# Seven block products in three of eight K pairs instead of two, with one block sum made by an accumulating transfer

## The chip, the cores and the metric

The kernel runs on one core of one Trainium2 chip. The metric is device time in microseconds (us), the median of the runs shown; lower is better. The core has a matrix engine (PE, with its weight loads shown as PEld), a vector engine (DVE), a scalar engine (ACT), a general engine (POOL) and a sequencer that mostly issues transfers (SP). Each engine works through its own instructions in order and waits on semaphores for the others.

## What is computed

Two decoder layers over 256 tokens of width 2048: a state-space mixer in the first, differential attention in the second, and after each a SwiGLU feed-forward network (FFN) with 5632 hidden columns, all with RMSNorm before and after. The change lies in the gate and up products of the FFN:

```python
def swiglu(h, w_gate, w_up, w_down):
    return (jax.nn.silu(h @ w_gate) * (h @ w_up)) @ w_down
...
    for i in range(DEPTH):
        ...
        h = rmsnorm(x, norm_ffn_pre[i])
        x = x + rmsnorm(swiglu(h, ffn_w_gate[i], ffn_w_up[i], ffn_w_down[i]), norm_ffn_post[i])
```

## The kernel before, in words

All weights come from HBM as float32. PE multiplies float32r, so each block of weights is split on the way: ACT casts it to `hi` (line 119), DVE subtracts to get `lo` (line 120), and a product is three matmuls: x_hi by hi, x_hi by lo, x_lo by hi.

**Where the blocks live.** A `raw` tile holds four blocks of 128x512 (1 MB) and there are three of them; `hi` and `lo` have four tiles each in the FFN. SP issues the loads in order and stops at one whose `raw` tile is still in use.

**The FFN.** Hidden columns come in chunks of 512. Chunk 10 is done by the plain routine `mv`. The other ten go two at a time through `pair`, once for gate (`wg`) and once for up (`wu`), so each FFN calls `pair` ten times and the kernel twenty times. The calls lie in three parts: one gate and up, then two, then two; each part is followed by its share of the down product (`out_proj`). What `pair` computes is a 2x2 grid of results: two token halves t by two column chunks c, each a PSUM accumulator `acc` (four banks). Its K dimension of 2048 is walked in eight K pairs kp = 0..7; each loads the 2x2 weight blocks (two K blocks by two chunks), and each of the four results needs two products of 128x128 by 128x512.

**The seven.** For the K pairs named in `SEVEN` the eight products are replaced by seven, after Strassen's scheme in Winograd's form. The block sums of x are made once per FFN by `make_forms` and kept in `xr` tiles (four); they are read through `form`. The sums of weight blocks are made per K pair: three raw blocks are split first (`prep(raw[:, 1:4])`), then DVE makes four sums in place of the raw blocks (lines 239 to 242, each 128x512), then the tile is split again (`prep(raw)`), giving `sh` and `sl`. Four of the seven products collect in banks of their own (`p1`, `p5`, `p6`, `p7`, tile name `cp`, from the four `aux` banks), the other three go straight into `acc`. After the last K pair of `SEVEN`, DVE combines the four (lines 257 to 260), and at the end of the pair `done` adds each to its `acc` and frees the bank (lines 743, 752, 753).

**What sets the order.** A scheduler places each engine's instructions by the order in which the kernel names them and by when tiles come free; `later` and `tick` delay some work by a number of steps. So the order of DVE and SP around a pair's end is not written in the source.

Of the kernel before, what the change touches and what calls it, by code (L numbers as in the profile page):

```python
# [10 lines left out]
F32 = mybir.dt.float32  # L11
F32R = mybir.dt.float32r
AF = mybir.ActivationFunctionType
ALU = mybir.AluOpType
AX = mybir.AxisListType

P = 128
S = 256
NT = 2
# [10 lines left out]
LAG = 4  # L30
LAG2 = 2

SEVEN = (3, 5)


@with_exitstack
def trunk_kernel(ctx, tc, x_rows, x_cols, vec_cols, vec64, post_rows, lam_rows,
                 w_zxbc, w_dt, w_so, w_qkv, w_ao,
                 w_g0, w_u0, w_d0, w_g1, w_u1, w_d1, out):
    nc = tc.nc  # L40
# [99 lines left out]
    def later(k, fn):  # L140
        deferred.append((step_no[0] + k, fn))
# [6 lines left out]
    def lookup(dct, key):  # L148
        while key not in dct:
            deferred.popleft()[1]()  # L150
        return dct[key]
# [49 lines left out]
    def pair(blocks, seven, form, done):  # L201

        flush()
        acc = {}  # L210
        end = len(blocks) - 1

        def mm(k, st, hi, lo, last):
            first = k not in acc
            if first:
                acc[k] = (auxp.tile([P, 512], F32, tag="aux", name="cp") if isinstance(k, str) else
                          accp.tile([P, 512], F32, tag="acc", name="acc"))
            for q, (a, b) in enumerate(((st[0], hi), (st[0], lo), (st[1], hi))):
                nc.tensor.matmul(acc[k], a, b, start=first and q == 0, stop=last and q == 2)  # L219

        ss = {}
        for kp, src in enumerate(blocks):
            raw = rawp.tile([P, 4, 512], F32, tag="raw", name="raw")
            for c in range(2):
                nc.sync.dma_start(raw[:, 2 * c:2 * c + 2], src[c])
            if kp not in seven:
                hi, lo = prep(raw)
                for t in range(NT):
                    for c, e in ((0, 2), (1, 0)):
                        for j in range(2):  # L230
                            mm((t, c), x_stat(2 * kp + j, t), hi[:, e + j], lo[:, e + j], kp == end and j == 1)
                        if kp == end:
                            done(t, c, acc[(t, c)], ss)
                    tick()
                continue
            last = kp == seven[-1]
            hi, lo = prep(raw[:, 1:4])

            nc.vector.tensor_tensor(raw[:, 2], raw[:, 2], raw[:, 0], op=ALU.add)
            nc.vector.tensor_tensor(raw[:, 0], raw[:, 0], raw[:, 1], op=ALU.add)  # L240
            nc.vector.tensor_tensor(raw[:, 1], raw[:, 1], raw[:, 2], op=ALU.add)
            nc.vector.tensor_tensor(raw[:, 3], raw[:, 3], raw[:, 1], op=ALU.add)
            sh, sl = prep(raw)
            k0, k1 = 2 * kp, 2 * kp + 1
            mm("p1", x_stat(k0, 0), hi[:, 1], lo[:, 1], last)
            mm((0, 0), x_stat(k1, 0), hi[:, 2], lo[:, 2], False)
            mm((0, 1), form(kp, 3), hi[:, 0], lo[:, 0], False)
            tick()
            mm("p6", form(kp, 2), sh[:, 1], sl[:, 1], last)
            mm("p5", form(kp, 0), sh[:, 2], sl[:, 2], last)  # L250
            mm("p7", form(kp, 1), sh[:, 0], sl[:, 0], last)
            mm((1, 0), x_stat(k1, 1), sh[:, 3], sl[:, 3], False)
            tick()
            if last:
                s1, u, w, x = (t512(n) for n in ("s1", "su", "sw", "sx"))
                nc.scalar.copy(s1, acc["p1"])
                nc.vector.tensor_tensor(u, acc["p6"], s1, op=ALU.subtract)
                nc.vector.tensor_tensor(w, acc["p5"], u, op=ALU.add)
                nc.vector.tensor_tensor(u, acc["p7"], u, op=ALU.add)
                nc.vector.tensor_tensor(x, acc["p7"], w, op=ALU.add)  # L260
                ss.update({(0, 0): (s1, ALU.add), (0, 1): (w, ALU.add), (1, 0): (u, ALU.subtract), (1, 1): (x, ALU.add)})

    def split(dst_hi, dst_lo, src):
        nc.scalar.copy(dst_hi, src)
        nc.vector.tensor_tensor(dst_lo, src, dst_hi.bitcast(F32), op=ALU.subtract)
# [399 lines left out]
    def t512(name, shape=(P, 512)):  # L665
        return t5.tile(list(shape), F32, tag="t512", name=name)
# [11 lines left out]

    def xr_tile(name):
        return postp.tile([P, 2, 512], F32, tag="xr", name=name, bufs=4)

    def fetch_x(src):
        for t in range(NT):
# [16 lines left out]
    def ffn(wg, wu, wd, step, final):  # L702
        acts, gt, forms = {}, {}, {}

        def rs(t):
            return lookup(rstd, (step - 1, t))

        def g_evac(t, ps):
            gt[(t, 10)] = t512("g")
            nc.scalar.activation(gt[(t, 10)], ps, AF.Silu, scale=rs(t))  # L710

        def u_evac(t, ps):
            g = gt[(t, 10)]
            nc.vector.scalar_tensor_tensor(g, ps, rs(t), g, op0=ALU.mult, op1=ALU.mult)
            acts[(t, 10)] = act_piece(g, f"f{step}_10_{t}")

        def make_forms(n):

            xf = []
            for t in range(NT):  # L720
                xf.append(t512("xf", (P, 4, P)))
                sl = slice(t * P, (t + 1) * P)
                nc.vector.tensor_tensor(xf[t], xT_hi[n][:, :, sl].bitcast(F32), xT_lo[n][:, :, sl].bitcast(F32), op=ALU.add)
            fa, fb = (t512("f", (P, 2, 2, P)) for _ in range(2))
            nc.vector.tensor_tensor(fa[:, 0], xf[1][:, 0:4:2], xf[1][:, 1:4:2], op=ALU.subtract)
            nc.vector.tensor_tensor(fa[:, 1], xf[1][:, 0:4:2], xf[0][:, 0:4:2], op=ALU.subtract)
            nc.vector.tensor_tensor(fb[:, 0], xf[0][:, 0:4:2], fa[:, 0], op=ALU.subtract)
            nc.vector.tensor_tensor(fb[:, 1], xf[0][:, 1:4:2], fb[:, 0], op=ALU.subtract)
            fh = postp.tile([P, 4, 2, P], F32R, tag="xr", name="fh", bufs=4)
            fl = postp.tile([P, 4, 2, P], F32R, tag="xr", name="fl", bufs=4)  # L730
            for k, f in enumerate((fa, fb)):
                split(fh[:, 2 * k:2 * k + 2], fl[:, 2 * k:2 * k + 2], f)
            forms[n] = (fh, fl)

        def form(kp, f):
            fh, fl = lookup(forms, kp // 2)
            return fh[:, f, kp % 2], fl[:, f, kp % 2]

        def g_done(p):
            def done(t, c, ps, ss):  # L740
                g, op = ss[(t, c)]
                gt[(t, 2 * p + 1 - c)] = g
                nc.vector.tensor_tensor(g, ps, g, op=op)
                nc.scalar.activation(g, g, AF.Silu, scale=rs(t))
            return done

        def u_done(p):
            def done(t, c, ps, ss):
                ch = 2 * p + 1 - c
                g = gt[(t, ch)]  # L750
                y, op = ss[(t, c)]
                nc.vector.tensor_tensor(y, ps, y, op=op)
                nc.vector.scalar_tensor_tensor(g, y, rs(t), g, op0=ALU.mult, op1=ALU.mult)

                def piece():
                    acts[(t, ch)] = act_piece(g, f"f{step}_{ch}_{t}")
                later(2, piece)
            return done

        def twos(w, c):  # L760
            return [[w[c + e, kp // 2, :, kp % 2 * 2:kp % 2 * 2 + 2] for e in range(2)] for kp in range(8)]

        mv([wg[10, k] for k in range(4)], u_stat, g_evac, LAG)
        for t in range(NT):
            rs(t)
            for h in range(2):
                nc.sync.dma_start(xr_d[t][h].rearrange("p (e k) -> p e k", e=2), xr_of[(t, h)])
        for k, n in enumerate(sorted({kp // 2 for kp in SEVEN})):
            later(1 + 3 * k, lambda n=n: make_forms(n))
        mv([wu[10, k] for k in range(4)], u_stat, u_evac, LAG2)  # L770
        parts = [(10, 0, 1), (2, 3, 4, 5), (6, 7, 8, 9)]
        for pi, part in enumerate(parts):
            for c in part:
                if c < 10 and c % 2 == 0:
                    pair(twos(wg, c), SEVEN, form, g_done(c // 2))
                    pair(twos(wu, c), SEVEN, form, u_done(c // 2))
            last = pi == len(parts) - 1
            if last:
                fetch_x(lambda t, h: xr_d[t][h].rearrange("p (e k) -> p e k", e=2))
            out_proj(wd, pi == 0, last, acts, [2 * c + e for c in part for e in range(2)], step, final, LAG2, t512,  # L780
                     load_post(step) if last else None)

    ffn(w_g0, w_u0, w_d0, 1, False)


# [182 lines left out]
```

## Time and profile before

| what | value |
|---|---|
| median of 3 runs | 2602.59 us (2600.7 to 2604.3) |
| the profiled execution, its own time | 2600.35 us |
| its span from first to last instruction | 2598.3 us |
| PE busy | 2561.4 us, 99% of the span |
| DVE busy | 1815.8 us, 70% |
| ACT busy | 1276.9 us, 49% |
| POOL busy | 158.4 us, 6% |
| DMA of the load queue | 489.27 MB, 53.3% of 16 engines' span |
| granted PE clock | 0.995 |

A timeline row of the profile gives start, duration, engine, line, operation, what it writes and reads, and in brackets how long the engine stood idle before it and who ended that. A row of groups ends in: busy us, mean ns of one, then idle us of the engine before them with the releasers. A row of waits gives total us, how often, and the longest. Rows of windows give the length, then busy us and (count) of PE, PEld, DVE, ACT and POOL, then the granted clock, the DMA share and GB/s. A matmul's duration in the trace includes its passage through the array, so matmuls overlap: their step is read from their starts.

### The profile page before, as it was taken

To read this page: it belongs to the slowest core of one execution; us is meant where nothing else is said; L and a number is where in the kernel's file an instruction comes from. 1 tells how busy PE (TensorE), PEld (TensorE's weight loads), DVE (VectorE), ACT (ScalarE), POOL (GpSimd) and SP (SyncE) were. 2 spreads that over 40 slices of the span, in tenths; PEclk is the share of its full clock that TensorE was granted. 3 is DMA by queue.
4 is the path that set the end of the run, shared out by engine and by line. 5 is a ranking of instruction groups with operands and counts; after the bars stand their busy time and mean duration, and the time that the engine had idled before them with its cause. 6 is when DMAs were issued, how large, how long until landed. Compare 5 with 4: busy or idle time off the path is not lost.

```text
span 2598.3 us, 31297 instructions
## 1 busy us (share of the span) xinstructions
PE 2561.4 (99%) x12270; PEld 2105.6 (81%) x12270; DVE 1815.8 (70%) x2230; ACT 1276.9 (49%) x1506; POOL 158.4 (6%) x164
## 2 busy tenths in 40 slices
PE   8999999999999999999999999999999999999998
PEld 7878888888878888888888788887788888888886
DVE  7888757887687567846785666556577478657864
ACT  4555655555564444534453554445554444434442
POOL 2021000111100000000001100001100000000001
PEclk9999999999999999999999999999999999999999
DMA  6545554544754654655465544444555555555563
GB/s 223 189 142 201 183 194 174 194 167 162 267 214 163 222 199 162 220 187 202 168 243 203 189 145 167 174 157 144 212 188 207 179 203 189 203 181 191 198 231 137
DMA packets 111699, 492.10 MB, mean 189 GB/s; under 512 B 10880, under 2 KB 27584, under 8 KB 75712
## 3 DMA queue, kind: packets, MB, share of 16 engines
q1 hardware_dynamic: 110896, 489.27, 53.3%
q8 instruction: 96, 1.57, 0.2%
q10 hardware_dynamic: 656, 0.85, 0.1%
q14 instruction: 51, 0.42, 0.0%
HBM read 483.71 MB, written 6.36 MB: 189 GB/s over the span
## 4 chain that ended last, share of the span: by engine, by line
PE 86%; DVE 6%; issue 3%; ACT 2%; DMA 2%; POOL 0%; DVEq 0%; SPq 0%; ACTq 0%; POOLq 0%
PE acc L168 39%; PE acc L219 23%; PE acc L193 11%; PE acc L195 6%; PE cp L219 3%; DVE lo L120 2%; ACT hi L119 2%; PE sc L844 1%; DMA raw<-in_w_d_dram 1%; DMA raw<-in_w_g_dram 1%; PE py L498 1%; DVE v L423 1%; PE pt_f L271 1%; PE ptx L574 0%; PE pyt L508 0%
## 5 line engine op out<-in xcount | busy, mean ns | idle before, releaser
L120 DVE TENSOR_TENSOR lo<-raw,hi 128x2048 fp32r<-128x2048 f32 (+2 forms) x528 | 1030.4, 1961 | 609.2 <-ACT hi L119 608.8
L119 ACT CAST hi<-raw 128x2048 fp32r<-128x2048 f32 (+2 forms) x528 | 851.1, 1618 | 924.8 <-PE acc L168 250.4
L219 PE MATMUL acc<-hi,xT 128*128 128x512 f32 x2080 | 656.8, 390 | 0.0
L193 PE MATMUL acc<-xT,hi 128*128 128x512 f32 x1280 | 456.6, 401 | 0.0
L219 PEld LDWEIGHTS acc<-hi,xT 128*128 128x128 f32 x2080 | 390.5, 188 | 80.5
L219 PE MATMUL acc<-lo,xT 128*128 128x512 f32 x1040 | 405.0, 389 | 0.0
L195 PE MATMUL acc<-xT,lo 128*128 128x256 f32 x1280 | 359.7, 282 | 5.8 <-DVE lo L120 5.8
L168 PE MATMUL acc<-hi,xT 128*128 128x512 f32 x1024 | 334.9, 399 | 2.3 <-ACT xT L579 2.0
L193 PEld LDWEIGHTS acc<-xT,hi 128*128 128x128 f32 x1280 | 241.8, 189 | 57.1 <-issue 0.9
L168 PE MATMUL acc<-hi,ah_f 128*128 128x512 f32 x704 | 274.8, 390 | 0.0
L168 PE MATMUL acc<-lo,ah_f 128*128 128x512 f32 x704 | 274.6, 390 | 0.0
L168 PE MATMUL acc<-hi,al_f 128*128 128x512 f32 x704 | 273.8, 389 | 0.0
L195 PEld LDWEIGHTS acc<-xT,lo 128*128 128x128 f32 x1280 | 243.4, 190 | 8.3 <-DVE lo L120 6.7
L168 PEld LDWEIGHTS acc<-hi,xT 128*128 128x128 f32 x1024 | 191.8, 188 | 48.1 <-issue 5.1
L219 PEld LDWEIGHTS acc<-lo,xT 128*128 128x128 f32 x1040 | 195.3, 188 | 40.2
L168 PE MATMUL acc<-lo,xT 128*128 128x512 f32 x512 | 206.7, 404 | 1.6 <-DVE lo L120 1.6
L168 PEld LDWEIGHTS acc<-hi,ah_f 128*128 128x128 f32 x704 | 132.2, 188 | 27.3
L168 PEld LDWEIGHTS acc<-hi,al_f 128*128 128x128 f32 x704 | 132.2, 188 | 27.0
L168 PEld LDWEIGHTS acc<-lo,ah_f 128*128 128x128 f32 x704 | 132.2, 188 | 26.9
L600 POOL TENSOR_TENSOR m<-m,wpost 128x512 f32<-128x512 f32 x24 | 44.2, 1842 | 1462.8 <-ACT junk L282 1423.2
L124 DVE SCALAR_TENSOR_TENSOR lo<-raw,cols,hi 128x512 fp32r<-128x512 f32 x128 | 92.7, 771 | 52.0 <-ACT hi L123 51.7
L168 PEld LDWEIGHTS acc<-lo,xT 128*128 128x128 f32 x512 | 96.4, 188 | 23.7 <-issue 3.9
(251 smaller groups left out, 2701.0 us busy)
## 6 DMA issues: line engine op xcount, KB each, us to landing
raw<-in_w_d_dram SPq DMA_DIRECT2D x88, 1024.0 KB, 4.8
raw<-in_w_zxbc_dram SPq DMA_DIRECT2D x80, 1024.0 KB, 4.8
raw<-in_w_g_dram SPq DMA_DIRECT2D x160, 512.0 KB, 4.4
raw<-in_w_u_dram SPq DMA_DIRECT2D x160, 512.0 KB, 4.7
raw<-in_w_qkv_dram SPq DMA_DIRECT2D x48, 1024.0 KB, 4.7
raw<-in_w_so_dram SPq DMA_DIRECT2D x32, 1024.0 KB, 4.7
raw<-in_w_ao_dram SPq DMA_DIRECT2D x16, 1024.0 KB, 4.7
mt<-acum_d SPq DMA_DIRECT2D x16, 512.0 KB, 6.9
```

The source lines that it names most:

```text
L119: nc.scalar.copy(hi, raw)
L120: nc.vector.tensor_tensor(lo, raw, hi.bitcast(F32), op=ALU.subtract)
L124: nc.vector.scalar_tensor_tensor(lo[:, j], raw[:, j], scale[j], hi[:, j].bitcast(F32), op0=ALU.mult, op1=ALU.subtract)
L168: nc.tensor.matmul(acc[t], a, b[:, j], start=(i == 0 and j == 0 and q == 0), stop=(i == last and j == 1 and q == 2))
L193: nc.tensor.matmul(acc[ct], hi[:, j, cs], x.rearrange("p a s -> p (a s)"), start=(i == 0 and j == 0), stop=False)
L195: nc.tensor.matmul(acc[ct][:, :S], lo[:, j, cs], x[:, 0], start=False, stop=(i == last and j == 1))
L219: nc.tensor.matmul(acc[k], a, b, start=first and q == 0, stop=last and q == 2)
L271: nc.tensor.transpose(pt[:, j], src[:, j * P:(j + 1) * P], ident)
L423: nc.vector.scalar_tensor_tensor(v, u[:, k:k + S], cwh[:, ch, k:k + 1], v, op0=ALU.mult, op1=ALU.add)
L498: nc.tensor.matmul(py[e * 64:(e + 1) * 64, a], xd[c][:, 2 * a + e], mts[c][:, 2 * a + e], start=True, stop=True)
L600: (nc.vector if n == 3 else nc.gpsimd).tensor_tensor(dst, mt, pw(n), op=ALU.mult)
L844: nc.tensor.matmul(sc[c][:, h], qT[cp, h, ts], kT[cp, h, :nk * P], start=True, stop=True)
```

## The change

`SEVEN` names K pairs 2, 4 and 6 instead of 3 and 5. For those, after the two loads of the `raw` tile, POOL issues a third transfer that reads one weight block again from HBM and adds it into block 0 of the tile. With that sum there, DVE makes three sums instead of four: the first adds the transferred sum to block 2, the other two are derived from it. The products use the same sums under new block numbers. `make_forms`, which made the x sums for two K pairs at once into two tiles, becomes `make_form` for one K pair into one tile, so three `xr` tiles are used instead of four.

```diff
-SEVEN = (3, 5)
+SEVEN = (2, 4, 6)
...
             for c in range(2):
                 nc.sync.dma_start(raw[:, 2 * c:2 * c + 2], src[c])
+            if kp in seven:
+                nc.gpsimd.dma_start(raw[:, 0:1], src[0][:, 1:2], accum_op=ALU.add)
...
             hi, lo = prep(raw[:, 1:4])
             nc.vector.tensor_tensor(raw[:, 2], raw[:, 2], raw[:, 0], op=ALU.add)
-            nc.vector.tensor_tensor(raw[:, 0], raw[:, 0], raw[:, 1], op=ALU.add)
-            nc.vector.tensor_tensor(raw[:, 1], raw[:, 1], raw[:, 2], op=ALU.add)
-            nc.vector.tensor_tensor(raw[:, 3], raw[:, 3], raw[:, 1], op=ALU.add)
+            nc.vector.tensor_tensor(raw[:, 3], raw[:, 3], raw[:, 2], op=ALU.add)
+            nc.vector.tensor_tensor(raw[:, 1], raw[:, 2], raw[:, 1], op=ALU.subtract)
             sh, sl = prep(raw)
...
-            mm("p6", form(kp, 2), sh[:, 1], sl[:, 1], last)
-            mm("p5", form(kp, 0), sh[:, 2], sl[:, 2], last)
+            mm("p6", form(kp, 2), sh[:, 2], sl[:, 2], last)
+            mm("p5", form(kp, 0), sh[:, 1], sl[:, 1], last)
...
-        def make_forms(n):
+        def make_form(kp):
...
-            fh = postp.tile([P, 4, 2, P], F32R, tag="xr", name="fh", bufs=4)
-            fl = postp.tile([P, 4, 2, P], F32R, tag="xr", name="fl", bufs=4)
...
+            ff = forms[kp] = xr_tile("ff", (P, 4, 2, P), F32R)
+            split(ff[:, :, 0], ff[:, :, 1], f)
...
-        for k, n in enumerate(sorted({kp // 2 for kp in SEVEN})):
-            later(1 + 3 * k, lambda n=n: make_forms(n))
+        for k, kp in enumerate(SEVEN):
+            later(1 + 3 * k, lambda kp=kp: make_form(kp))
```

In the orders below a row is line, operation, out<-in and shape; `lo_...` and `hi_...` are the split blocks (2048 columns: a whole tile; 1536: the three raw blocks of a seven), `su`, `sw`, `sx` and `s_...` the combinations of the four separate products. Line numbers in the changed kernel's `pair` run two or three higher.

DVE before, at the end of the first gate pair of the first FFN, from the last seven (K pair 5) to the combinations:

```order
L120 TENSOR_TENSOR lo_7238<-raw,hi_7237 128x1536
L239 TENSOR_TENSOR raw<-raw 128x512
L240 TENSOR_TENSOR raw<-raw 128x512
L241 TENSOR_TENSOR raw<-raw 128x512
L242 TENSOR_TENSOR raw<-raw 128x512
L120 TENSOR_TENSOR lo_7246<-raw,hi_7245 128x2048
L120 TENSOR_TENSOR lo_7283<-raw,hi_7282 128x2048
L120 TENSOR_TENSOR lo_7314<-raw,hi_7313 128x2048
L257 TENSOR_TENSOR su<-cp,s_7270 128x512
L258 TENSOR_TENSOR sw<-cp,su 128x512
```

The same place on DVE in the changed kernel, from the last seven (now K pair 6):

```order
L120 TENSOR_TENSOR lo_7276<-raw,hi_7275 128x1536
L242 TENSOR_TENSOR raw<-raw 128x512
L243 TENSOR_TENSOR raw<-raw 128x512
L244 TENSOR_TENSOR raw<-raw 128x512
L120 TENSOR_TENSOR lo_7283<-raw,hi_7282 128x2048
L120 TENSOR_TENSOR lo_7320<-raw,hi_7319 128x2048
L120 TENSOR_TENSOR lo_7359<-raw,hi_7358 128x2048
L259 TENSOR_TENSOR su<-cp,s_7307 128x512
L260 TENSOR_TENSOR sw<-cp,su 128x512
```

A seven has three sums instead of four. In both orders two whole tiles are split between the last seven and the combinations; before they are K pairs 6 and 7, now K pair 7 and the first of the next pair. The first sum (line 242 in the changed kernel) is the only instruction of DVE that waits for the accumulating transfer; what stands behind it on DVE waits with it.

POOL before, from the norms ahead of the first FFN to the down product's end:

```order
L600 TENSOR_TENSOR m<-m,wpost 128x512 x6
L88 TENSOR_TENSOR rs_post_0_6587<-ms_post_0_6585,mhalf 128x1
L88 TENSOR_TENSOR rs_pre_0_6681<-ms_pre_0_6679,mhalf 128x1
L88 TENSOR_TENSOR rs_post_1_6726<-ms_post_1_6724,mhalf 128x1
L88 TENSOR_TENSOR rs_pre_1_6816<-ms_pre_1_6814,mhalf 128x1
L600 TENSOR_TENSOR m<-m,wpost 128x512 x6
```

POOL in the changed kernel from the same norms:

```order
L88 TENSOR_TENSOR rs_post_0_6587<-ms_post_0_6585,mhalf 128x1
L88 TENSOR_TENSOR rs_pre_0_6681<-ms_pre_0_6679,mhalf 128x1
L88 TENSOR_TENSOR rs_post_1_6726<-ms_post_1_6724,mhalf 128x1
L88 TENSOR_TENSOR rs_pre_1_6816<-ms_pre_1_6814,mhalf 128x1
L228 DMA raw<-in_w_g_dram 128x512 x3
L228 DMA raw<-in_w_u_dram 128x512 x3
```

Three issues for every call of `pair` now stand on POOL, thirty for each FFN, ahead of the six multiplications of the down product's last part. Each waits for the loads of its `raw` tile.

More of the change, by code (lines that the diff above doesn't have):

```diff
@@ L677, in load_post, with xr_tile @@
         return get
-    def xr_tile(name):
-        return postp.tile([P, 2, 512], F32, tag="xr", name=name, bufs=4)
+    def xr_tile(name, shape=(P, 2, 512), dtype=F32):
+        return postp.tile(list(shape), dtype, tag="xr", name=name, bufs=4)
     def fetch_x(src):
@@ L715, in u_evac @@
             acts[(t, 10)] = act_piece(g, f"f{step}_10_{t}")
-        def make_forms(n):
-            xf = []
+        def make_form(kp):
+            n, k = kp // 2, kp % 2 * 2
+            xf = t512("xf", (P, NT, 2, P))
+            f = t512("f", (P, 4, P))
             for t in range(NT):
-                xf.append(t512("xf", (P, 4, P)))
                 sl = slice(t * P, (t + 1) * P)
[L723 to L728, printed above, removed]
-            fh = postp.tile([P, 4, 2, P], F32R, tag="xr", name="fh", bufs=4)
-            fl = postp.tile([P, 4, 2, P], F32R, tag="xr", name="fl", bufs=4)
-            for k, f in enumerate((fa, fb)):
-                split(fh[:, 2 * k:2 * k + 2], fl[:, 2 * k:2 * k + 2], f)
-            forms[n] = (fh, fl)
+                nc.vector.tensor_tensor(xf[:, t], xT_hi[n][:, k:k + 2, sl].bitcast(F32),
+                                        xT_lo[n][:, k:k + 2, sl].bitcast(F32), op=ALU.add)
+            nc.vector.tensor_tensor(f[:, 0], xf[:, 1, 0], xf[:, 1, 1], op=ALU.subtract)
+            nc.vector.tensor_tensor(f[:, 1], xf[:, 1, 0], xf[:, 0, 0], op=ALU.subtract)
+            nc.vector.tensor_tensor(f[:, 2], xf[:, 0, 0], f[:, 0], op=ALU.subtract)
+            nc.vector.tensor_tensor(f[:, 3], xf[:, 0, 1], f[:, 2], op=ALU.subtract)
+            ff = forms[kp] = xr_tile("ff", (P, 4, 2, P), F32R)
+            split(ff[:, :, 0], ff[:, :, 1], f)
         def form(kp, f):
-            fh, fl = lookup(forms, kp // 2)
-            return fh[:, f, kp % 2], fl[:, f, kp % 2]
+            ff = lookup(forms, kp)
+            return ff[:, f, 0], ff[:, f, 1]
         def g_done(p):
```

## The prediction

> **What bounds the kernel now.** I read the busy shares of the page first, then the chain that ended last, then the windows over four calls of `pair` that follow each other.
>
> ```profile
> PE 2561.4 (99%) x12270; PEld 2105.6 (81%) x12270; DVE 1815.8 (70%) x2230; ACT 1276.9 (49%) x1506; POOL 158.4 (6%) x164
> PE 86%; DVE 6%; issue 3%; ACT 2%; DMA 2%; POOL 0%; DVEq 0%; SPq 0%; ACTq 0%; POOLq 0%
> 926.41:968.65 42.24, 42.24 (x188) 34.96 (x188) 31.78 (x25) 20.37 (x15) 0.00 (x0) 1.00 0.53 189
> 968.65:1011.00 42.35, 42.35 (x190) 35.10 (x189) 31.94 (x29) 19.90 (x14) 0.00 (x0) 1.00 0.56 198
> 1011.00:1053.40 42.40, 42.13 (x193) 34.59 (x192) 34.93 (x32) 20.87 (x16) 0.00 (x0) 1.00 0.51 181
> 1053.40:1095.80 42.40, 42.40 (x189) 35.13 (x188) 31.21 (x26) 20.98 (x15) 0.00 (x0) 1.00 0.55 192
> sum 169.39, PE 169.12 PEld 139.78 DVE 129.86 ACT 82.13 POOL 0.00; mean PE 42.28 PEld 34.95 DVE 32.46 ACT 20.53 POOL 0.00
> ```
>
> PE is never idle in a pair (169.12 of 169.39 us), so a matmul taken away there is time gained, as long as the split blocks arrive. The engine next to it is DVE: 129.86 us of 169.39, 77%, not the 70% of the whole span. POOL is empty here.
>
> A matmul's row says 0.39 us; what it costs PE is the step between starts. First and eighteenth matmul of a seven:
>
> ```profile
> 790.75 0.39 PE L219 MATMUL cp<-hi,xT 128*128 128x512 f32 x1
> ...
> 794.60 0.39 PE L219 MATMUL cp<-hi,fl 128*128 128x512 f32 x1
> ```
>
> Seventeen steps in 3.85 us: 0.2265 us each. So an ordinary K pair takes PE 24 x 0.2265 = 5.44 us, a seven 21 x 0.2265 = 4.76 us.
>
> **Step 1, matmuls removed.** One more seven per call, three matmuls less, twenty calls: 60 x 0.2265 = **13.6 us**, all on PE and so all on the path. (By the rows' 0.39 us it would be 23.4 us, which is the overlap counted twice.)
>
> **Step 2, DVE work.** One seven on DVE and its neighbours in the second window:
>
> ```profile
> 981.47 2.29 DVE L120 TENSOR_TENSOR lo<-raw,hi 128x2048 fp32r<-128x2048 f32 x1 [2.14 <-ACT hi L119]
> 986.48 1.76 DVE L120 TENSOR_TENSOR lo<-raw,hi 128x1536 fp32r<-128x1536 f32 x1 [2.72 <-ACT hi L119]
> 988.28 0.69 DVE L239 TENSOR_TENSOR raw<-raw 128x512 f32<-128x512 f32 x1
> ...
> 990.46 0.69 DVE L242 TENSOR_TENSOR raw<-raw 128x512 f32<-128x512 f32 x1
> 993.20 6.70 DVE L120 TENSOR_TENSOR lo<-raw,hi 128x2048 fp32r<-128x2048 f32 x3 [2.05 <-ACT hi L119]
> ```
>
> Busy time of a seven before: 1.76 + 4 x 0.69 + 2.29 = 6.81 us; with three sums 6.12 us; an ordinary K pair 2.29 us. A call before: 6 x 2.29 + 2 x 6.81 = 27.36; after: 5 x 2.29 + 3 x 6.12 = 29.81; **+2.45 us** per call. The third seven also brings a third stretch of 2.05 us in which DVE stands still between its last sum and the second split, because ACT's cast of the sums lies between and the order puts nothing there:
>
> ```profile
> ACT hi L119 <- DVE raw L242: 181.9, 40, 5.4
> SPq L225 <- DVE lo L120: 705.6, 156, 12.6
> ```
>
> Does DVE still keep up? Over the four windows it is idle for 169.39 - 129.86 = 39.5 us, of which 8 x 2.05 = 16.4 are those stretches; 23.1 are spare. After: 4 x 2.45 = 9.8 more work, 4 x 2.05 = 8.2 more standing, and the four calls shorter by 4 x 0.68 = 2.7. That leaves 23.1 - 20.7 = **2.4 us spare in 167**. DVE is thus filled to 98.5%. Not all of the 2.4 can be used: at a pair's end DVE waits for ACT, which waits for a load whose `raw` tile had just come free, about 1 us each time:
>
> ```profile
> 1003.90 1.91 ACT L119 CAST hi<-raw 128x2048 fp32r<-128x2048 f32 x1 [1.76 <-DMA raw<-in_w_g_dram]
> 1005.85 2.29 DVE L120 TENSOR_TENSOR lo<-raw,hi 128x2048 fp32r<-128x2048 f32 x1 [0.96 <-ACT hi L119]
> ```
>
> Four of those are 3.8 us against 2.4 spare: 1.4 us short per four calls. The four `hi`/`lo` tiles let DVE start a part up to three blocks ahead, which covers some. I take 0.4 us lost per stretch of four calls; there are four such (two in each FFN), so **1.6 us lost**. The ends: 0, if the lead covers it; 4 x 2 = 8 us, if the waits at a pair's end double.
>
> **Step 3, the accumulating transfer.** It moves 256 KB on POOL's queue, and no row shows such a transfer. Before it may be issued its `raw` tile must have landed; the first sum waits for it; `prep(raw[:, 1:4])` does not. Nearest rows, the transfers' issues with KB and median us to landing, then one with its spread and the length of an issue on SP:
>
> ```profile
> raw<-in_w_g_dram SPq DMA_DIRECT2D x160, 512.0 KB, 4.4
> raw<-in_w_u_dram SPq DMA_DIRECT2D x160, 512.0 KB, 4.7
> mt<-acum_d SPq DMA_DIRECT2D x16, 512.0 KB, 6.9
> wpost<-in_post_rows_dram SPq DMA_DIRECT2D x18, 256.0 KB, 4.9
> out_dram<-x SPq DMA_DIRECT2D x8, 256.0 KB, 2.1
> DMA to landing us min/median/max: 3.1/4.9/9.1
> L225 SPq DMA_DIRECT2D raw<-in_w_u_dram x160: 327/328/1585, 801.5 to 2472.3; - x160
> ```
>
> The nearest is `wpost` (min, median and max are its): same 256 KB, same 128x512, from HBM into the core beside the weight loads. With the usual issue, 0.33 + 4.9 = **5.2 us**. Ends: 0.33 + 2.1 = 2.4 us and 1.59 + 9.1 = 10.7 us; the addition, which no row prices, speaks for the upper half.
>
> What covers it: three `raw` tiles, so the load for a seven at K pair k is issued when DVE has split k-3, as the row of SP's waits above says. Until it reaches the first sum of k, DVE has k-2 (a seven), k-1 and the first split of k ahead of it. By the starts above a seven takes 993.20 - 986.48 + 6.70/3 = 8.95 us, less one sum's step of 0.73: 8.2; then 2.2 and 1.8. That is 12.2 us, less 4.7 for the load: **7.5 us of cover even when DVE never waits for PE**. 5.2 fits under 7.5, so the transfer costs nothing. If the cover were short by e, the next seven's load would already be on its way and profit from the delay, so about every second seven would pay: 30 x e.
>
> The Trainium skill ("DMA: Bandwidth & Descriptors", Anatomy of one DMA — SWDGE (gpsimd) path) gives about 2.0 us plus the bytes over 436 GB/s for a transfer issued there, which I estimate at 2.6 us; the sum would be the same and the chance of a late transfer smaller. No run here shows it yet, and `wpost` at 4.9 us is nearly twice that, so I leave the chance as the rows give it.
>
> **Smaller edits together.** `make_form` does three halves of what `make_forms` did twice and runs under the plain `mv` of chunk 10, where DVE idles 2.55 us before a single split (row below): nothing. POOL's waits hold up nobody, since POOL has no other work between the norms and the down product's last part: its last row before the pairs is at 742.91 and none follows until 1100. The reload of the residual, which before waited on SP for the tiles of the x sums, is spread out; it sat idle for 11.0 us in four waits, behind loads that had their own wait, so nothing either way. The combinations move one K pair closer to `done`; they take DVE from 999.81 to 1002.60, 2.8 us, against 5.44 us of PE's last K pair: nothing. The added bytes, 60 x 256 KB on 489 MB, are 3%: nothing at a DMA share of 0.55.
>
> ```profile
> 767.45 2.29 DVE L120 TENSOR_TENSOR lo<-raw,hi 128x2048 fp32r<-128x2048 f32 x1 [2.55 <-ACT hi L119]
> 742.91 0.55 POOL L88 TENSOR_TENSOR rs_pre<-ms_pre,mhalf 128x1 f32<-128x1 f32 x1 [7.97 <-DVE ms_pre L85]
> SPq L688 <- PE cp L219: 11.0, 4, 4.4
> 999.81 0.68 DVE L257 TENSOR_TENSOR su<-cp,s 128x512 f32<-128x512 f32 x1
> ...
> 1002.60 2.28 DVE L120 TENSOR_TENSOR lo<-raw,hi 128x2048 fp32r<-128x2048 f32 x1
> ```
>
> **The sum.** -13.6 + 1.6 = -12.0 us. The profiled execution took 2600.35 us, so 2588.4; it stands 2.2 us under the median of 2602.59, and against that the forecast is **2590.6 us**.
>
> **The rivals.**
>
> *The transfer is late* (slower). One mechanism at one place: DVE's first sum waits for POOL's transfer. It decides from 30 x e = 12, e = 0.4, a transfer of 7.9 us in all. For it speak the 9.1 us that one `wpost` took and the reading of the destination that an addition needs; against it the median of 4.9. At 1.59 + 6.9 = 8.5 us e is 1.0, 30 us lost: 2590.6 + 30 = 2621; at 10.7 us e is 3.2, 96 us: 2687.
>
> *DVE becomes the bound* (little gained). The 98.5% above is an average; if the full 2 us per stretch of four calls are missing, 8 us are lost: 2602.6 - 13.6 + 8 = 2597. For it speaks the margin of 2.4 us; against it that PE waits for nothing now, so there is a lead to use up.
>
> *POOL's issue is held up by DVE* (no gain). If POOL can prepare a transfer only while DVE is not in an operation, the issue waits for the end of one, up to a split's 2.29 us: 5.2 + 2.3 = 7.5 us, just the cover, and with part of the sevens over it by 0.2 to 0.5 us, 6 to 15 us lost: about 2600. POOL does nothing in a pair, so the nearest row is its multiplication in the down product, the same shape each time:
>
> ```profile
> L600 POOL TENSOR_TENSOR m<-m,wpost x24: 1287/1302/2783, 669.2 to 2571.3; 128x512 f32<-128x512 f32 x24
> ```
>
> The longest is 1.5 us over the median, so POOL can be held up; but the median is 15 ns over the shortest, so it mostly isn't, and 5.2 + 1.5 = 6.7 us still fits under 7.5: a small chance.
> The Trainium skill ("SBUF — State Buffer", Who interferes with whom) says that DVE and POOL share a pair of ports by an exclusive lock, that a DVE operation with two inputs there blocks POOL's reads, and that descriptors of POOL's transfers starve behind DVE's two-port modes. Here it would give the time just named; the spread of that row agrees that POOL is held up at times.
>
> *The gain does not appear*, because PE's idle time turns up elsewhere: the chain is PE at 86% and the stages around are PE-bound too, so hardly.
>
> **How the numbers follow.** Chances: forecast 0.65, transfer late 0.18, DVE the bound 0.10, POOL held up 0.05, no gain 0.02. A change under 0.2% (5.2 us) can't be told from none here. Faster by more: the forecast and a third of DVE the bound, 0.68; within: the other two thirds, half of POOL held up and the last, 0.11; slower: the late transfer and the rest, 0.21. The range: low 2602.6 - 13.6 - 3 (run to run) = 2586; above, up to a transfer of 8.2 us, e = 0.7, 21 us: 2612. Outside lie most of the late transfers. The forecast's own range is 2586 to 2599 (0 to 8 us lost).
>
> **What the next profile would show.** Step 1: 3660 matmuls at line 219 instead of 3720 at a step of 0.2265. Step 2: DVE near 98% in windows over four calls and single short waits of PE for `lo` at second gate and up pairs. Step 3: landing of the transfers near 5 us and hardly any idle time before line 242. Wrong would be: DVE idle before line 242 for tens of us, PE waiting for `lo` in every pair, a landing above 7.9 us.

## The result and the profile after

The changed kernel takes **2586.62 us** (median of 4 runs, 2585.26 to 2587.95), the kernel before 2601.64 us (4 runs) in the same comparison: ratio 0.9941, 95% interval 0.9926 to 0.9956, 15.0 us faster. The forecast was 2590.6 us. The profiled execution took 2586.13 us with a span of 2584.3 us.

Busy time, the chain that ended last, and two of the four stretches in which four calls of `pair` follow each other, each from its first to its last matmul:

```profile
PE 2549.0 (99%) x12210; PEld 2096.6 (81%) x12210; DVE 1851.3 (72%) x2280; ACT 1300.4 (50%) x1524; POOL 213.2 (8%) x224
PE 94%; DVE 3%; issue 1%; ACT 1%; POOL 0%; DMA 0%; DVEq 0%; POOLq 0%; ACTq 0%
927.20:1095.42 168.22, 168.22 (x751) 138.93 (x750) 137.66 (x120) 86.53 (x61) 9.61 (x11) 1.00 0.66 211
2058.30:2226.53 168.23, 168.23 (x751) 138.92 (x750) 137.68 (x120) 87.69 (x61) 9.60 (x11) 1.00 0.64 211
```

The same two stretches in the kernel before:

```profile
926.41:1097.43 171.02, 170.75 (x760) 140.80 (x759) 131.49 (x111) 82.18 (x57) 0.00 (x0) 1.00 0.54 192
2065.88:2237.76 171.88, 171.39 (x761) 140.83 (x759) 131.87 (x111) 82.17 (x57) 0.00 (x0) 1.00 0.54 191
```

PE is busy for the whole of each stretch, DVE does some 6 us more, and the stretch is about 3 us shorter. Over the six parts of the program that consist of `pair` calls, PE's time from first to last matmul fell from 855.39 to 840.13 us, 15.26 us less; the rest of the span grew by 1.3 us. So the gain is where the change is.

The first of DVE's three sums and the accumulating transfer in the changed kernel (durations min/median/max, then what the instruction's engine waited for; from the transfer's view, KB each and median us from the start of its issue to landing):

```profile
L242 DVE TENSOR_TENSOR raw<-raw x60: 678/692/694, 778.2 to 2467.6; 128x512 f32<-128x512 f32 x60
  DMA raw<-in_w_u_dram: 0.2, 1
L228 POOL DMA_DIRECT2D raw<-in_w_g_dram x30: 866/872/1060, 767.3 to 2421.1; - x30
DMA to landing us min/median/max: 3.5/3.8/9.1
raw<-in_w_g_dram POOLq DMA_DIRECT2D x30, 256.0 KB, 3.8
raw<-in_w_u_dram POOLq DMA_DIRECT2D x30, 256.0 KB, 3.8
```

Of 60 sums one waited for its transfer, 0.2 us. In the median the transfer lands 3.8 us after the start of its issue, of which POOL is busy for 0.87.

### The profile page after: what moved, and what is told of

Same layout as the page of the kernel before. It is cut to its first block, busy times and chain, and to the rows that moved or that the text cites. A ratio compares the mean times of both kernels' runs of the same rounds, so it can differ in the third digit from the quotient of the medians.

```text
span 2584.3 us, 31682 instructions
## 1 busy us (share of the span) xinstructions
PE 2549.0 (99%) x12210; PEld 2096.6 (81%) x12210; DVE 1851.3 (72%) x2280; ACT 1300.4 (50%) x1524; POOL 213.2 (8%) x224
## 4 chain that ended last, share of the span: by engine, by line
PE 94%; DVE 3%; issue 1%; ACT 1%; POOL 0%; DMA 0%; DVEq 0%; POOLq 0%; ACTq 0%
PE acc L168 40%; PE acc L219 26%; PE acc L193 11%; PE cp L219 6%; PE acc L195 6%; PE sc L844 1%; PE pt_f L273 1%; PE py L500 1%; DVE v L425 1%; DVE lo L120 0%; ACT hi L119 0%; PE ptx L576 0%; PE pyt L510 0%; PE po L879 0%; PE pyo L533 0%
## 5 line engine op out<-in xcount | busy, mean ns | idle before, releaser
L120 DVE TENSOR_TENSOR lo<-raw,hi 128x2048 fp32r<-128x2048 f32 (+2 forms) x548 | 1060.7, 1952 | 558.3 <-ACT hi L119 556.8
L119 ACT CAST hi<-raw 128x2048 fp32r<-128x2048 f32 (+2 forms) x548 | 876.8, 1612 | 882.3 <-DVE raw L244 226.3
L219 PE MATMUL acc<-hi,xT 128*128 128x512 f32 x1840 | 589.1, 390 | 0.0
L219 PEld LDWEIGHTS acc<-hi,xT 128*128 128x128 f32 x1840 | 345.2, 188 | 71.3
L219 PE MATMUL acc<-lo,xT 128*128 128x512 f32 x920 | 358.0, 389 | 0.0
L168 PE MATMUL acc<-hi,xT 128*128 128x512 f32 x1024 | 336.3, 400 | 2.3 <-ACT xT L581 1.9
L168 PEld LDWEIGHTS acc<-hi,xT 128*128 128x128 f32 x1024 | 192.8, 189 | 48.6 <-issue 5.1
L168 PE MATMUL acc<-lo,xT 128*128 128x512 f32 x512 | 207.7, 406 | 1.6 <-DVE lo L120 1.6
L219 PEld LDWEIGHTS acc<-lo,xT 128*128 128x128 f32 x920 | 172.7, 188 | 35.7
L219 PE MATMUL cp<-hi,ff 128*128 128x512 f32 x360 | 120.7, 389 | 0.0
L168 PEld LDWEIGHTS acc<-lo,xT 128*128 128x128 f32 x512 | 97.0, 189 | 24.1 <-issue 3.9
```

Of the source, the lines that this page charges most:

```text
L119: nc.scalar.copy(hi, raw)
L120: nc.vector.tensor_tensor(lo, raw, hi.bitcast(F32), op=ALU.subtract)
L168: nc.tensor.matmul(acc[t], a, b[:, j], start=(i == 0 and j == 0 and q == 0), stop=(i == last and j == 1 and q == 2))
```

## Experiments

The runs were made in three groups, each with its own runs of the kernel before: 2600.91 us (19 runs) beside the two halves and the delays of ten and thirty memsets with a scratch tile; 2602.2 us (19) beside the four sevens, the early cast, both together and the delay of two memsets with a scratch tile; 2602.11 us (13) beside the last four. Each ratio is to the kernel before in the same group.

### The two halves of the change, each alone

Two sevens as before, but with the transfer and three sums:

```diff
-SEVEN = (2, 4, 6)
+SEVEN = (3, 5)
```

> Two sevens per call as before (K pairs 3 and 5), but with the accumulating transfer and three DVE sums. Theory (PE is the bound, a seven is worth 3 matmuls x 0.2265 us, relieving DVE is worth nothing by itself): no matmul less than before, so 2601.6 us, at most 2 us less if the small PE stalls at the ends of calls go with the relief. Rival (DVE was a hidden bound and the transfer is what gained): 5 us or more below before, 2596 or less.

Measured: 2603.97 us (11 runs), ratio 1.0011 [1.0002, 1.002]. The transfer by itself gains nothing. The sums did wait for it, all ten times at K pair 3 of the up products, where at its issue two or three loads are under way besides the last one of its own tile, and it lands after 7.9 us (median of the ten) instead of 3.8 as at K pair 5. What DVE waited ahead of its first sums, then what PE waited for DVE:

```profile
  DMA raw<-in_w_u_dram: 26.1, 10
PE pt_f L273 <- DVE sw L753: 7.0, 6, 2.0
```

DVE's lead covered most of these 26 us: in the pairs' part of the program PE waited for DVE only in a few transposes of the activation, 7.0 us in the second row and 1.1 us in another, and that in the longest of the 11 runs (2610.25 us), which is the profiled one.

Three sevens, but four sums on DVE and no transfer:

```diff
-                nc.gpsimd.dma_start(raw[:, 0:1], src[0][:, 1:2], accum_op=ALU.add)
...
+            nc.vector.tensor_tensor(raw[:, 0], raw[:, 0], raw[:, 1], op=ALU.add)
```

> Three sevens, but all four block sums made by DVE and no transfer. DVE stands idle for 168.06 - 137.50 = 30.6 us in four calls of the changed kernel, 25.3 of them while ACT casts the sums: 5.3 us spare. Twelve more sums at 0.73 us are 8.8 us, so 3.5 us short per stretch of four calls. Theory (the transfer is what keeps DVE under PE): 4 x 3.5 = 14 us lost at most, less what DVE's lead covers: 2592 to 2601 us, with PE waiting for lo in the later calls. Rival (DVE's lead covers it all, the transfer is not needed): 2587 us as the changed kernel.

Measured: 2608.13 us (9 runs), ratio 1.0026 [1.0016, 1.0036], 21.5 us over the changed kernel and above every time that was expected. The first of the stretches of four calls, the large splits of DVE in it with the idle time ahead of them, and what PE waited for in the pairs:

```profile
926.06:1099.47 173.41, 169.96 (x750) 138.37 (x749) 144.57 (x129) 84.77 (x60) 0.00 (x0) 1.00 0.51 184
L120 DVE TENSOR_TENSOR lo<-raw,hi 128x2048 fp32r<-128x2048 f32 x31 | 70.1, 2288 | 24.7 <-ACT hi L119 24.6
PE acc L219 <- ACT hi L119: 12.2, 16, 1.1
```

DVE has 144.57 us of work there against 137.66, and the stretch takes 173.41 us instead of 168.22, although PE has the same matmuls. A seven's stand is the time in which DVE stands idle between its last sum and the second split; twelve of them are 24.6 us (second row). Work and stands make 144.6 + 24.6 = 169.2 of the 173.4 us: DVE sets the pace. Of the other 4.2 us, 2.45 are one wait in the first call, ahead of the split at 938.70, and the rest are pauses of under 0.2 us between instructions; from the second call on DVE waits nowhere but in its stands. So neither half is worth anything alone: the third seven takes work from PE that DVE can only follow when the fourth sum is taken from DVE, and the transfer frees time on DVE that only the third seven can use.

### Four sevens, and an attempt to fill DVE's stand

```diff
-SEVEN = (2, 4, 6)
+SEVEN = (2, 4, 5, 6)
```

> The changed kernel with a fourth seven per call, at K pairs 2, 4, 5 and 6. By the theory that DVE's work and its standing set how many sevens pay: of four calls (168.06 us) DVE has 5.3 us spare; four more sevens of 6.12 us and 2.11 standing for ordinary pairs of 2.29 add 23.8, and the calls should be 2.7 shorter, so 21 us are missing, and four calls take about 186 us instead of 165; with 5 such stretches the kernel is at 2586.6 + 5 x 18.4 = about 2680 us, PE waits for ACT and DVE in every call, and the first sum hardly ever waits for the transfer. By the rival, that PE has slack enough because DVE's standing is filled with the next pair's work, it is 13.6 us faster than the changed kernel, 2573. By the rival that late transfers are the cost, DVE's idle time ahead of the first sum grows instead.

Measured: 2693.11 us (4 runs), ratio 1.0351 [1.0336, 1.0367]; the account of DVE's work and stand said about 2680.

```profile
935.73:1123.92 188.19, 173.65 (x738) 137.36 (x737) 149.79 (x132) 91.37 (x64) 13.09 (x15) 0.98 0.61 190
PE cp L219 <- ACT hi L119: 53.4, 41, 2.2
```

DVE's 149.79 us and sixteen stands of 2.1 us make 183.4 of 188.19 us (186 were forecast). Only one of the 80 first sums waited for its transfer, 0.4 us, so late transfers are not the cost. In this order of instructions the idle time of DVE inside a seven is no reserve.

Next, the block that the transfer makes is cast and subtracted alone, ahead of the three sums' blocks, with three sevens:

```diff
-            sh, sl = prep(raw)
+            nc.scalar.copy(sh[:, 0], raw[:, 0])
+            nc.vector.tensor_tensor(sl[:, 0], raw[:, 0], sh[:, 0].bitcast(F32), op=ALU.subtract)
+            nc.scalar.copy(sh[:, 1:4], raw[:, 1:4])
+            nc.vector.tensor_tensor(sl[:, 1:4], raw[:, 1:4], sh[:, 1:4].bitcast(F32), op=ALU.subtract)
```

> The changed kernel, but the block that the transfer makes is cast and subtracted by itself ahead of the other three, so that DVE has 0.7 us of work in the 2.1 us in which it stands in a seven. Theory: PE is the bound and has no wait in a pair, so the time stays within 0.2% of the changed kernel's 2586.6 (2583 to 2591), while DVE's spare time over four calls grows by about 12 x 1.1 = 13 us less the extra starts. Rival: single short waits of DVE still cost PE something at the calls' ends; then 2 to 4 us faster.

Measured: 2608.89 us (10 runs), ratio 1.0028 [1.0018, 1.0037]: 22 us slower than the changed kernel, against both expectations. DVE around a seven's end late in a stretch (lines 250 and 252 are the two new subtractions; 242 to 244 the sums), then the cast on ACT that DVE's last wait is for, and the loads on SP:

```profile
2176.00 2.29 DVE L120 TENSOR_TENSOR lo<-raw,hi 128x2048 fp32r<-128x2048 f32 x1 [1.29 <-ACT hi L119]
2178.21 1.75 DVE L252 TENSOR_TENSOR lo<-raw,hi 128x1536 fp32r<-128x1536 f32 x1
...
2183.48 0.69 DVE L244 TENSOR_TENSOR raw<-raw 128x512 f32<-128x512 f32 x1
2188.43 2.29 DVE L120 TENSOR_TENSOR lo<-raw,hi 128x2048 fp32r<-128x2048 f32 x1 [4.26 <-ACT hi L119]
2186.49 1.91 ACT L119 CAST hi<-raw 128x2048 fp32r<-128x2048 f32 x1 [5.29 <-DMA raw<-in_w_g_dram]
2178.32 0.99 SPq L225 DMA_DIRECT2D raw<-in_w_g_dram  x2
2179.99 1.53 SPq L225 DMA_DIRECT2D raw<-in_w_u_dram  x2
```

The scheduler now puts the next K pair's split (2176.00) ahead of the seven's last subtraction (2178.21). Each of the two frees a `raw` tile when it ends, so SP issues two loads at 2178.32 and two more at 2179.99. With these four under way, the first two, which are for the last K pair, have landed only at 2186.4, some 8 us after 2178.32; ACT waits 5.29 us for them, and DVE 4.26 us. Over the whole run 21 of the pairs' 320 loads took more than 7 us to land, against 5 in the changed kernel. The rows show this order and this wait; that the whole 22 us come from such places was not tested apart.

Both together:

> The early cast and four sevens (2, 4, 5, 6) together. By the theory of DVE's standing, a seven's standing falls from 2.1 to about 1.0: over four calls 16 x 1.1 = 17.6 of the 21 us that were missing come back, so about 3.5 us are lost per four calls of the 2.7 won: 2586.6 - 13.6 + 5 x 3.5 = about 2590, between 2573 (DVE just keeps up) and 2605 (its waits at the calls' ends are lost too). By the rival that DVE's standing is no cost, it equals the run with four sevens and no early cast.

Measured: 2595.24 us (10 runs, 2589.71 to 2601.88), ratio 0.9978 [0.9966, 0.999]. With four sevens the early cast gives back 98 us, which fits the account that DVE's stands were their cost; the forecast of about 2590 was near. The kernel is 0.2% faster than before, and slower than the changed kernel.

### How much cover the transfer has

Here POOL gets some work between the landing of a `raw` tile and the issue of the transfer: two operations on one element, and a number of small memsets between them.

```diff
+                nc.gpsimd.tensor_tensor(scr[:, 0:1], raw[:, 0, 0:1], raw[:, 0, 0:1], op=ALU.mult)
+                for _ in range(10):
+                    nc.gpsimd.memset(scr, 0.0)
+                nc.gpsimd.tensor_tensor(scr[:, 1:2], raw[:, 0, 0:1], scr[:, 2:3], op=ALU.mult)
                 nc.gpsimd.dma_start(raw[:, 0:1], src[0][:, 1:2], accum_op=ALU.add)
...
+    scr = postp.tile([P, 104], F32, tag="scr", name="scr", bufs=1)
```

Ten memsets:

> The changed kernel with POOL kept busy for some 2.5 us (ten memsets of 104 columns and two tiny operations) between the landing of the raw tile and the issue of the accumulating transfer. Theory (cover of 7.5 us from the landing to the first sum, of which the transfer uses 0.9 + 3.8 at most): 7.2 us at most, still covered: 2586.6 us as the changed kernel. Rival (DVE is so full that any delay shows): 60 x 0.5 to 60 x 2.5, 30 to 150 us more.

Thirty memsets:

> The same with thirty memsets, some 6.5 us of delay: 10.3 to 11.2 us from the landing to the sum, 2.8 to 3.7 us over the cover of 7.5. Theory (every second seven pays, 30 x e): 84 to 111 us more, 2671 to 2698 us, DVE idle ahead of its first sum in about every second seven. Rival 1 (every seven pays): 168 to 222 us more. Rival 2 (the cover is larger than worked out): under 2600 us.

Measured: 2698.46 us (ratio 1.0393 [1.0359, 1.0426]) with a median delay of 3.5 us (2.5 had been planned), 2848.24 us (ratio 1.095 [1.0932, 1.0968]) with 9.3 us (6.5 planned). That is 112 and 262 us over the changed kernel; the second is above every time that was expected. Two memsets were tried next:

> The changed kernel with two small memsets on POOL and two one-element operations between a load's landing and the transfer's issue: about 1.0 to 1.5 us of delay, a third of the delay that cost 112 us. By the margins that the changed kernel's trace has between landing and first sum (median 4.6 us, 10 of 60 under 1.5 us, nearly all of these at K pair 2), a delay of 1.0 to 1.5 us costs the sum of what is missing, 3 to 6 us: 2589 to 2593. By the prediction's cover of 7.5 us it costs nothing: 2586. By a rival in which a short wait also lowers the clock or POOL's operations disturb DVE, it costs a third of the longer delay's loss, about 35 us: 2620.

Measured: 2645.45 us, ratio 1.0172 [1.0141, 1.0204]: 59 us lost with 1.5 us of delay, above all three expectations. Something else had changed: in all three kernels the median step between matmuls is 0.234 us from 650 us on, 0.227 in the changed kernel. The longer step begins ahead of the first delay, with the first matmuls that read the `hi` and `lo` tiles allocated behind the scratch tile. The tile moved those allocated behind it, `hi` and `lo` among them. So the delays were repeated with the scratch elements in a filler tile (`gap0`) that the kernel has anyway; each engine's order but POOL's is the same as in the changed kernel.

> The same delay as in the first run with a delay of about 1.5 us (two memsets, two one-element operations on POOL), but the scratch elements lie in a filler tile that the kernel already has, so no tile moves. In the earlier delay kernels the scratch tile of 416 bytes per partition was put in ahead of others, and the matmuls' step in their traces is 0.234 us from 650 us on, against 0.227 in the changed kernel. Theory: that step, 3.1% of the 1890 us of matmuls behind it, was 58 us of the loss, and the delay itself cost next to nothing: 2586.6 + 6.3 (the sum of what 1.5 us exceed the margins that the changed kernel's trace shows between landing and first sum) = 2593 at most, 2587 if DVE's spare time covers it. Rival, that the delay itself cost the 59 us: 2645 again.

> Five memsets, about 2.3 us of delay, scratch in the filler tile. By the margins 17 us are missing between landings and first sums; DVE has about 5.3 us spare per four calls, 26 in all, so between 0 and 17 us lost: 2587 to 2604. By the prediction's cover of 7.5 us less 3.8 of landing, 3.7 us are free and it costs nothing. Rival, the delay itself cost what the earlier kernels lost: about 2665.

> Ten memsets, about 3.5 us of delay, scratch in the filler tile. By the margins 39 us are missing; with some of it absorbed by DVE's spare time 20 to 45 us lost: 2607 to 2632; the earlier kernel less 58 us for the longer step gives 2640. By the prediction's cover, 7.5 less 3.8, it just fits: 2587. Rival, the delay itself cost it all: 2698 again.

| memsets | delay, median | time | over the changed kernel |
|---|---|---|---|
| 0 (changed kernel) | 0 | 2586.62 us | |
| 2 | 1.4 us | 2607.13 us (10 runs, 2590.65 to 2624.1), ratio 1.0014 [0.9991, 1.0037] | 20.5 us |
| 5 | 2.3 us | 2648.62 us (4 runs), ratio 1.0189 [1.0151, 1.0227] | 62.0 us |
| 10 | 3.5 us | 2677.08 us (4 runs), ratio 1.0288 [1.0272, 1.0303] | 90.5 us |

The two runs with two memsets differ by 38 us; their median delays are 1.5 and 1.4 us, so nearly all of it is the scratch tile's place. But even the clean delays cost two to four times what is missing from the changed kernel's margins (6, 17 and 39 us); those expectations fell too. The same transfer, the fifteenth, in the changed kernel and with five memsets shows why. Its issue on POOL, the next loads on SP, and the sum that needs it, changed kernel first:

```profile
1032.74 0.87 POOL L228 DMA_DIRECT2D raw<-in_w_g_dram  x1 [12.12 <-DMA raw<-in_w_g_dram]
1035.36 0.81 SPq L225 DMA_DIRECT2D raw<-in_w_g_dram  x2
1039.23 0.69 DVE L242 TENSOR_TENSOR raw<-raw 128x512 f32<-128x512 f32 x1
```

Five memsets:

```profile
1046.29 0.80 SPq L225 DMA_DIRECT2D raw<-in_w_g_dram  x2
1046.56 0.89 POOL L232 DMA_DIRECT2D raw<-in_w_g_dram  x1 [0.30 <-POOL gap L231]
1054.43 0.69 DVE L246 TENSOR_TENSOR raw<-raw 128x512 f32<-128x512 f32 x1 [4.34 <-DMA raw<-in_w_g_dram]
```

In the changed kernel the transfer leads the next load by 2.6 us and lands after 3.62 us. Delayed, it comes 0.3 us after that load and lands after 7.77 us, and DVE waits 4.34 us for it. Transfer by transfer it is the same: with no load in flight at its issue, the 27 of this kernel land after 3.77 us (median); the 13 that were issued between the two loads of a tile, with no other in flight, land after 7.81, and DVE waits for every one of them, 2.7 to 5.5 us. The other 20 were issued while earlier loads were still landing, and land after 4.1 us in the median (3.6 to 7.4). With ten memsets the first two groups are 3.79 us (24) and 7.61 (20); in the changed kernel one of 60 falls between, and it is the longest of its landings, 9.1 us.

Of the 13 late transfers 12 are at K pair 6, where the changed kernel has 3.5 us between landing and first sum (median), not at K pair 2, where it has least. So the wait is less a matter of so many tenths of a microsecond missing than of the transfer's place among the loads. A small lead is not enough either: in the run with two sevens, nine of the ten transfers that DVE waited for were issued 0.1 to 1.3 us ahead of the next load, with two more under way.

And a wait on DVE grows on PE. With five memsets, at the same place:

```profile
1056.18 0.39 PE L219 MATMUL acc<-hi,ff 128*128 128x512 f32 x1
1058.57 0.50 PE L219 MATMUL cp<-hi,ff 128*128 128x512 f32 x1 [2.00 <-ACT hi L119]
1060.89 0.80 PE L219 MATMUL cp<-lo,ff 128*128 128x512 f32 x1 [1.82 <-DVE lo L120]
...
1064.90 0.63 PE L219 MATMUL acc<-lo,xT 128*128 128x512 f32 x1
1056.00:1061.00 5.00, 1.18 (x5) 0.44 (x3) 2.90 (x3) 4.38 (x4) 0.00 (x0) 0.83 0.00 2
1061.00:1064.00 3.00, 3.00 (x7) 2.37 (x8) 3.00 (x3) 1.60 (x1) 0.00 (x0) 0.50 0.72 250
1064.00:1068.00 4.00, 4.00 (x14) 3.15 (x13) 2.93 (x3) 1.51 (x1) 0.02 (x1) 0.74 1.00 357
```

After two idle times of 2.00 and 1.82 us with one matmul between them, the granted clock is 0.50 and a matmul's step 0.43 us. The last row's 0.74 over 4 us is 2.1 us at half clock, so it lasts until about 1066.1: 5.2 us of matmuls at half speed. So this late transfer costs 3.8 us of waiting and about 2.5 us of slow matmuls. Over the whole run the pairs take 63.4 us longer than in the changed kernel, and 38.8 of these are PE's waits; the rest fits the half clock. The Trainium skill ("TensorE: Matmul & The Clock Gate", Part 1: The HAM clock gate) says that the clock is halved after about 3.4 us of idleness and comes back after about as long a busy time. These rows agree in kind and roughly in size: by the 0.83 over 5 us half clock begins at about 1059.3, 2.7 us after the end of the last matmul ahead of the waits (1056.57), and it lasts for 5.2 us of matmuls.

Last, the place of the tiles alone: a tile of 448 bytes per partition, written once and never read, where the scratch tile of 416 had been, and no delay.

> The changed kernel with an unused tile of 448 bytes per partition (seven times 64) at the place where the delay kernels had 416 (six and a half times 64). Theory: the matmuls' step of 0.234 us came from weights that start 32 bytes off a multiple of 64; then this shift costs nothing, step 0.227, 2583 to 2590. Rival: any shift of the weights' tiles by a fraction of 512 bytes costs it: step 0.234 and about 2645.

Measured: 2621.28 us (4 runs), ratio 1.0074 [1.0059, 1.0089], 34.7 us over the changed kernel: the theory of multiples of 64 bytes fell, and the rival held, with a smaller size than it named. Matmuls by form, changed kernel, then the shifted one (min/median/max ns):

```profile
L219 PE MATMUL acc<-hi,xT x1840: 387/389/486, 776.7 to 2483.1; 128*128 128x512 f32 x184
L219 PE MATMUL cp<-hi,ff x360: 387/389/402, 790.1 to 2477.0; 128*128 128x512 f32 x180
L219 PE MATMUL acc<-hi,xT x1840: 391/394/483, 775.9 to 2516.1; 128*128 128x512 f32 x184
L219 PE MATMUL cp<-hi,ff x360: 388/389/398, 789.6 to 2509.9; 128*128 128x512 f32 x180
```

## Why the prediction was right

**The number.** The forecast was 12.0 us less, the measured gain is 15.0, and the time lies 0.6 us above the low end of the range, 2586. Of the 3.0 us between, the traces show 1.9: the pairs gained 1.6 us more by Step 1 and lost 1.6 us less by Step 2 than was forecast, and the rest of the span grew by 1.3 us. The other 1.1 is within the spread of the runs (2599.91 to 2604.3 us before, 2585.26 to 2587.95 after).

**Step 1, the matmuls.** Held. The trace has 3660 of them at line 219 at a median step of 0.227 us, and 13.6 of the 15.26 us that the pairs lost are theirs. The other 1.6 was not forecast. Most of it is PE's short waits in the pairs of before (171.02 less 170.75 and 171.88 less 171.39 in the rows above, 1.2 us over the four stretches), which are gone, since PE is busy throughout.

**Step 2, DVE.** The term was mis-sized: 1.6 us lost was forecast, none is. The account of spare time was nearly right. DVE's splits in the second stretch in the program, from 1184.30 to 1352.36, the idle time ahead of them last:

```profile
L120 DVE TENSOR_TENSOR lo<-raw,hi 128x2048 fp32r<-128x2048 f32 x31 | 69.9, 2287 | 25.4 <-ACT hi L119 25.2
L120 DVE TENSOR_TENSOR lo<-raw,hi 128x1536 fp32r<-128x1536 f32 x12 | 21.0, 1752 | 5.5 <-ACT hi L119 5.5
```

DVE is idle for 30.1 us of this stretch. Its twelve stands of 2.1 us make 25.2 of that (the first row), and 4.9 are left: 3.4 ahead of two small splits in the first two calls, and pauses of 0.1 us or less. (The 5.5 in the second row count 2.1 us ahead of a split that began before the stretch.) 2.3 of the 4.9 stem from one split that DVE had done before the stretch began, since 43 of its 44 are in it; that leaves 2.6 us spare against the 2.4 forecast. The step that failed is the next one, that waits of about 1 us at each pair's end would use this up and 0.4 us per stretch would reach PE. In the four stretches DVE has no such wait at a pair's end, and PE waits nowhere in the pairs. That is the lower end named, but not by its reason: nothing was there for the lead of the `hi`/`lo` tiles to cover. Where the spare time is gone, in the run with three sevens and no transfer, PE loses 5.2 us per stretch, and there too it is DVE's work and stands that it waits for. The forecast rival "DVE becomes the bound" is true of that kernel and not of this one.

**Step 3, the transfer.** That it costs nothing held; its reasons held in part, and it was partly luck. 5.2 us were taken from the nearest row, 3.8 were measured (0.33 of the 5.2 was counted twice, since that row's landing runs from the start of the issue). The estimate from the page "DMA: Bandwidth & Descriptors" of the Trainium skill, 2.6 us, is below every landing here. The cover of 7.5 us is about the right size in the median: from the start of the issue to the first sum the changed kernel has 9.0 us. But it is not one number. It ranges from 4.5 to 14.3 us, and it is thinnest at K pair 2 of the up calls, where two loads of the next tile are under way at the transfer's issue: there the ten sums come 4.5 to 7.0 us after the issue and 0.1 to 1.5 us after the landing. With the sevens at K pairs 3 and 5 the same transfer came too late ten times of 40, which the sum of the cover does not tell apart. Nor is the transfer one number. A delay of 2.3 us and a landing of 3.8, 6.1 together, would mostly have fitted, and yet cost 62 us, because 13 of the transfers landed only after 7.8 (median).

What the sum left out is that the transfer's own time depends on the loads beside it, and that the next loads are issued as soon as DVE frees a tile. The price of 30 x e did not hold either: with thirty memsets 56 of the 60 first sums came within 0.3 us of their transfer's landing, not every second, and a transfer between two loads lands 4 us later at once, whatever e is.

**Rivals.** The late transfer did not happen, but its point of decision was set too far out: not a transfer of 7.9 us, but one delayed by 1.4 us costs 20 us in the median (the ten runs spread over 33 us) and brings the time back to that of before. POOL held up by DVE did not happen either: the issues take 863 to 1060 ns, median 872, although DVE was in an operation during all or part of 51 of the 60. The rule cited for this rival speaks of POOL's reads where DVE has two inputs, as it has in a pair, and of descriptors only behind two-port modes, so it did not give that time for the issues. POOL's own operations do vary: the one-element operation after the memsets took 0.19 us at one place and 1.68 at another (five memsets):

```profile
1031.47 0.19 POOL L231 TENSOR_TENSOR gap<-raw,gap 128x1 f32<-128x1 f32 x1
1044.58 1.68 POOL L231 TENSOR_TENSOR gap<-raw,gap 128x1 f32<-128x1 f32 x1
```

DVE was idle by the end of the first and in a row of splits during the second; that DVE held it was not tested apart.

## What to carry to other kernels

Where one engine is full and the next is nearly so, two edits that are worth nothing alone can be worth the sum together: count what each takes from which engine before judging either. Whether a transfer beside a stream of loads is covered hung here on its place among the loads more than on a number of microseconds; look at what is under way at its issue, and at how soon the next load follows. Add scratch for an experiment where no other tile moves.

## What was not expected of the hardware

- **The place of tiles sets the matmul's step.** In the compiled programs the stationary `xT` and the moved `hi` and `lo` start a multiple of 512 bytes apart in the changed kernel, and the step is 0.227 us. With `hi` and `lo` moved by 448 bytes it is 0.233 to 0.234 where the stationary operand is `xT`, with 416 bytes 0.234 to 0.235. It is 0.233 also with the stationary `ah_f`, which had not moved. Where it is `ff`, which moved by the same amount, it stays at 0.227 in both. So the distance between the two counts here, not the address of one. Two shifts were tried; which distances are free is not known.
- **A transfer issued between a tile's two loads lands about 4 us later** than one issued with no load in flight: 7.6 to 7.8 us against 3.8.
- **Half clock after a wait of 3.8 us** on PE that one matmul interrupts, for about 5 us of matmuls.
